# Average pooling in 3D: the closing barrier and the clearing of semaphores run beside the last stores

## The chip, the cores and the metric

The kernel runs on one core of a Trainium2 chip. The metric is the device time of one execution in microseconds, as the median of several runs; smaller is better. The profile is that of one execution, and its span goes from the first to the last instruction of the kernel. The device time is longer than the span: the profiled execution took 93.1 us and its span is 91.3 us.

## The reference

The input `x` is a float32 array of 8 x 32 x 32 x 32 x 32 (batch, channels, depth, height, width). The output is the mean over windows of 2 x 2 x 2 that do not overlap, an array of 8 x 32 x 16 x 16 x 16:

```python
out_d = d // kernel_size
...
for i in range(out_d):
    for j in range(out_h):
        for k in range(out_w):
            ...
            result[:, :, i, j, k] = np.mean(window, axis=(-3, -2, -1))
```

So 33.55 MB are read and 4.19 MB are written, and each element read takes part in one sum.

## The kernel before

Batch and channels make 256 rows, taken as two tiles of 128 rows, one row on each of the 128 partitions of on-chip memory. A row's depth, height and width lie behind each other. The list `plan` cuts each tile's rows into pieces along the depth: six pieces of 4 MB (8192 floats in each partition), and two buffers more that are filled by two loads of 2 MB each. There are ten loads in all (line 77), all issued from SyncE, called SP here, into a pool of five buffers named `tin`. A load into a buffer that was used before waits until VectorE is done with the old contents.

For each piece VectorE runs three instructions, in `pool_unit`: it adds neighbours in depth (line 58), then neighbours in width (line 62), and then neighbours in height with the factor 0.125 (line 65); the last writes its part of `obuf`. The result of all pieces stays in two buffers `obuf` until whole runs of it are stored. There are three stores (line 86), issued from SP as well: 2 MB for the first tile, and 1.75 MB and 0.25 MB for the second. Each waits for the VectorE instruction that completes its source. The third can be issued only when the last piece is finished.

Semaphores connect the engines. Each load or store adds 16 to a semaphore, in sixteen single counts, when its data has landed. Nine semaphores are used in the body, numbers 99 to 107; 101 counts VectorE's instructions, and the other eight belong to transfers and are used in turn. The three stores add to 102, 103 and 104, each of which an earlier load has already raised to 16, so that a store has landed when its semaphore is at 32.

What the change is about lies behind the body. `tc.close()` and `tc.compile()` (lines 95 and 96) generate a closing block, and the profile puts its instructions down to line 96. In order:

- SP waits, in four instructions of two semaphores each, for all eight transfer semaphores, stores included; a drain of SP then waits for VectorE's count.
- A barrier over all five engines. ScalarE (ACT), TensorE (PE), VectorE (DVE) and SP each run a drain that adds 1 to semaphore 96, and then wait for semaphore 97. GpSimd (POOL) waits until 96 is at 4, takes the 4 away, and adds 4 to 97; each of the others takes 1 of it and goes on.
- GpSimd, after a drain, clears the range of semaphores 99 to 107 with one instruction.
- The same barrier again.

The kernel itself already reorders the program once: lines 101 to 108 take the first load out of the body and put it ahead of the opening barrier. Instructions of the opening carry line 125, that of the program's construction.

Of the kernel before, what the change touches and what calls it, by code (L numbers as in the profile page):

```python
# [1 line left out]

# [4 lines left out]

F32 = mybir.dt.float32
KF = 256

@with_exitstack
def pool_rows(
    ctx: ExitStack,
    tc: tile.TileContext,
    x: bass.AP,
    kernel_size: int,
    out: bass.AP,
):
    nc = tc.nc  # L20
    assert kernel_size == 2, "only kernel_size == 2 supported"

    B, C, D, H, W = x.shape
    P = nc.NUM_PARTITIONS
    assert (B * C, D, H, W) == (2 * P, 32, 32, 32)
    add = mybir.AluOpType.add

    xv = x.rearrange("b c d h w -> (b c) (d h w)")  # L30
    ov = out.rearrange("b c d h w -> (b c) (d h w)")

    pool_in = ctx.enter_context(tc.tile_pool(name="pin", bufs=5))
    pool_out = ctx.enter_context(tc.tile_pool(name="pout", bufs=1))
    obuf = [pool_out.tile([P, 16 * KF], F32, name=f"obuf{t}") for t in range(2)]
    dummy = pool_out.tile([P, 1], F32, name="dummy")

    plan = [
        (0, 0, (32,)),
        (0, 32, (32,)),
        (0, 64, (32,)),
        (0, 96, (32,)),
        (1, 0, (32,)),
        (1, 32, (32,)),
        (1, 64, (16, 16)),
        (1, 96, (16, 16)),  # L50
    ]

    def pool_unit(buf, t, k0, kb):

        od = kb // 8
        a = buf.rearrange("p (o dd e) -> p o dd e", o=od, dd=2)
        b = buf[:, :od * 1024]
        nc.vector.tensor_add(  # L58
            out=b.rearrange("p (o e) -> p o e", o=od), in0=a[:, :, 0], in1=a[:, :, 1])
        bv = b.rearrange("p (e ww) -> p e ww", ww=2)  # L60
        c = buf[:, od * 1024:od * 1536]
        nc.vector.tensor_add(out=c, in0=bv[:, :, 0], in1=bv[:, :, 1])  # L62
        cv = c.rearrange("p (j hh k) -> p j hh k", hh=2, k=16)
        o0 = k0 * KF // 8
        nc.vector.tensor_tensor_reduce(  # L65
            out=obuf[t][:, o0:o0 + od * 256].rearrange("p (j k) -> p j k", k=16),
            in0=cv[:, :, 0], in1=cv[:, :, 1],
            scale=0.125, scalar=0.0, op0=add, op1=add, accum_out=dummy[:, :],
        )

    for t, k0, parts in plan:
        tin = pool_in.tile([P, 32 * KF], F32, tag="tin", name="tin")
        views = []
        o = 0
        for kb in parts:
            v = tin[:, o * KF:(o + kb) * KF]
            nc.sync.dma_start(
                out=v, in_=xv[t * P:(t + 1) * P, (k0 + o) * KF:(k0 + o + kb) * KF])
            views.append((v, k0 + o, kb))
            o += kb  # L80
        for v, k, kb in views:
            pool_unit(v, t, k, kb)

    for t, k0, kb in [(0, 0, 16), (1, 0, 14), (1, 14, 2)]:
        nc.sync.dma_start(
            out=ov[t * P:(t + 1) * P, k0 * KF:(k0 + kb) * KF],
            in_=obuf[t][:, k0 * KF:(k0 + kb) * KF],
        )

def kernel(tc: tile.TileContext, x: bass.AP, kernel_size: int, out: bass.AP):
    nc = tc.nc
    pool_rows(tc, x, kernel_size, out)
    tc.close()
    tc.compile()  # L96
    blocks = nc.main_func.blocks

    opening, program = blocks[0].instructions, blocks[tc.starting_block_idx].instructions
    load = next(i for i in program if isinstance(i, mybir.InstDMACopy))
    assert load.engine == nc.sync.engine
    barrier = next(
        n for n, i in enumerate(opening)
        if i.engine == load.engine and isinstance(i, mybir.InstDrain))
    program.remove(load)
    opening.insert(barrier, load)

# [1 line left out]
_INS = ['x', 'kernel_size']  # L112
_OUTS = [((8, 32, 16, 16, 16), 'float32')]

_NUMBERS = {'kernel_size': 2}

# [26 lines left out]
```

## Time and profile before

| what | value |
|---|---|
| time, median of 3 runs | 93.52 us (93.45 to 93.53) |
| the profiled execution | 93.1 us |
| span in the profile | 91.3 us |
| VectorE busy | 64.0 us, 70% of the span |
| bytes over the span | 413 GB/s |
| VectorE waiting for loads | 20.5 us, 6 times |
| start of the last store's issue on SP | 85.2 us |
| issue to landing of the three stores | 36.2, 8.8 and 5.1 us |

The profile has one row for each engine that did work and one for the transfers, with one digit for each fortieth of the span (2.28 us): 9 means that nine tenths or more of that slice were busy. Semaphore instructions and drains are not counted as busy. They are still in the trace, as instructions of an engine's queue: a "q" behind the engine's name (SPq, POOLq) marks them, and their duration is that of the execution, without the wait ahead of it. The groups of one line, asked for within a window of time, show how many ran, their shortest, median and longest duration in nanoseconds, and the first and last start.

### The profile page before, as it was taken

To read this page: it belongs to the slowest core of one execution; us is meant where nothing else is said; L and a number is where in the kernel's file an instruction comes from. 1 tells how busy PE (TensorE), PEld (TensorE's weight loads), DVE (VectorE), ACT (ScalarE), POOL (GpSimd) and SP (SyncE) were. 2 spreads that over 40 slices of the span, in tenths; PEclk is the share of its full clock that TensorE was granted. 3 is DMA by queue.
4 is the path that set the end of the run, shared out by engine and by line. 5 is a ranking of instruction groups with operands and counts; after the bars stand their busy time and mean duration, and the time that the engine had idled before them with its cause. 6 is when DMAs were issued, how large, how long until landed. Compare 5 with 4: busy or idle time off the path is not lost.

```text
span 91.3 us, 103 instructions
## 1 busy us (share of the span) xinstructions
DVE 64.0 (70%) x40; POOL 0.2 (0%) x4
## 2 busy tenths in 40 slices
DVE  0000079974999299939995699749999999999300
POOL 0000000000000000000000000000000000000000
DMA  8998799999997899999997999989999999999992
GB/s 230 459 445 373 344 445 459 459 459 459 459 445 344 373 445 459 459 459 459 459 431 330 388 459 459 459 345 459 445 395 423 459 431 395 409 409 436 427 395 84
DMA packets 1872, 37.75 MB, mean 413 GB/s; under 512 B 208, under 2 KB 208, under 8 KB 336
## 3 DMA queue, kind: packets, MB, share of 16 engines
q1 hardware_dynamic: 1872, 37.75, 97.2%
HBM read 33.55 MB, written 4.19 MB: 413 GB/s over the span
## 4 chain that ended last, share of the span: by engine, by line
DMA 58%; DVE 35%; issue 0%; DVEq 0%
DMA tin<-in_x_dram 58%; DVE tin L58 19%; DVE tin L62 10%; DVE obuf L65 6%; DVE dummy L65 0%; DVEq L96 0%
## 5 line engine op out<-in xcount | busy, mean ns | idle before, releaser
L58 DVE TENSOR_TENSOR tin<-tin 128x4096 f32<-128x4096 f32 (+1 forms) x10 | 35.7, 3569 | 20.5 <-DMA tin<-in_x_dram 20.5
L62 DVE TENSOR_TENSOR tin<-tin 128x2048 f32<-128x2048 f32 (+1 forms) x10 | 18.6, 1864 | 0.3
L65 DVE CUSTOM_DVE_ANT_1 obuf<-tin 128x1024 f32<-128x1024 f32 (+1 forms) x10 | 10.1, 1011 | 0.3
L65 DVE DVE_READ_ACCUMULATOR2_ANT dummy<- 128x1 f32 x10 | 0.8, 82 | 0.0
L125 POOL MEMSET const-bfloat16-1.0<- 128x1 bf16 x1 | 0.1, 101 | 0.0
L125 POOL MEMSET const-uint8-127<- 128x1 uint8 x1 | 0.1, 101 | 0.0
L125 POOL MEMSET const-float32-0.0<- 128x1 f32 x1 | 0.1, 98 | 0.2 <-issue 0.2
L125 POOL MEMSET const-float32-1.0<- 128x1 f32 x1 | 0.1, 98 | 0.0
## 6 DMA issues: line engine op xcount, KB each, us to landing
tin<-in_x_dram SPq DMA_DIRECT2D x6, 4096.0 KB, 34.9
tin<-in_x_dram SPq DMA_DIRECT2D x4, 2048.0 KB, 38.0
out_dram<-obuf SPq DMA_DIRECT2D x1, 2048.0 KB, 36.2
out_dram<-obuf SPq DMA_DIRECT2D x1, 1792.0 KB, 8.8
out_dram<-obuf SPq DMA_DIRECT2D x1, 256.0 KB, 5.1
```

The source lines that it names most:

```text
L58: nc.vector.tensor_add(out=b.rearrange("p (o e) -> p o e", o=od), in0=a[:, :, 0], in1=a[:, :, 1])
L62: nc.vector.tensor_add(out=c, in0=bv[:, :, 0], in1=bv[:, :, 1])
L65: nc.vector.tensor_tensor_reduce(out=obuf[t][:, o0:o0 + od * 256].rearrange("p (j k) -> p j k", k=16), in0=cv[:, :, 0], in1=cv[:, :, 1], s ...
L125: nc = _bacc.Bacc("TRN2", target_bir_lowering=False, num_devices=1)
```

## The change

After the program has been generated, the changed kernel edits the closing block. The purpose is that the barrier and the clearing don't stand behind the landing of the stores.

- SP no longer waits for the three store semaphores on its way into the closing barrier. It still waits there for the semaphores of the loads and for VectorE's count.
- The first barrier stays. Behind it GpSimd clears the semaphores in two pieces, 99 to 101 and 105 to 107, each with a drain ahead of it, and leaves out 102, 103 and 104.
- The second barrier is removed.
- SP ends with three instructions, one for each store: it waits until the semaphore has 32 and subtracts 32, so that it is back at zero.

```diff
+    closing = blocks[-1].instructions
+    stores = [
+        i for i in program
+        if isinstance(i, mybir.InstDMACopy) and "out_" in i.outs[0].memref]
+    kept = [u.id for i in stores for u in i.sync_info.on_update]
+    final = next(
+        i for i in closing
+        if i.engine == nc.sync.engine and isinstance(i, mybir.InstDrain))
+    waits = {w.id: w for w in final.sync_info.on_wait}
+    closing[closing.index(final)] = mybir.InstDrain(
+        name=final.name, engine=final.engine, ins=[], outs=[], is_reset_sema=False,
+        sync_info=mybir.SyncInfo(
+            on_wait=[w for n, w in waits.items() if n not in kept], on_update=[]))
...
+    while len(closing) > reset:
+        closing.pop()
+    n = first
+    while n < stop:
+        m = n
+        while m < stop and m not in kept:
+            m += 1
+        if m > n:
+            closing.append(mybir.InstDrain(
+                name=nc.get_next_instruction_name(), engine=nc.gpsimd.engine, ins=[], outs=[],
+                is_reset_sema=True, reset_range_start=n, reset_range_stop=m))
+            nc.gpsimd.sem_clear(range(n, m))
+        n = m + 1
+    for n in kept:
+        w = waits[n]
+        closing.append(mybir.InstEventSemaphore(
+            name=nc.get_next_instruction_name(), engine=nc.sync.engine, ins=[], outs=[],
+            sync_info=mybir.SyncInfo(
+                on_wait=[w],
+                on_update=[mybir.SyncUpdate(
+                    sync_type="semaphore", id=n, ant_name=w.ant_name,
+                    update_mode="sem-sub-imm", update_value=w.wait_value)])))
```

`reset` is the place of the drain ahead of the clearing; the loop that pops removes all from there on, the second barrier included. At this point the waits of SP's drain are still in one list; they are split into instructions of at most two waits later, when the program is lowered.

## The prediction

> **What bounds the kernel now.** I read the page first, then busy times by stretch around the end, then the waits of the SP queue, then the closing block (line 96) in short windows. The page:
>
> ```profile
> span 91.3 us, 103 instructions
> DMA  8998799999997899999997999989999999999992
> DMA 58%; DVE 35%; issue 0%; DVEq 0%
> out_dram<-obuf SPq DMA_DIRECT2D x1, 256.0 KB, 5.1
> ```
>
> The row of tenths says that the transfers fill the span up to the last slice, which is at two tenths: there the DMA has stopped and something else runs. The chain of waits ends with the last VectorE work at 85.2 us, so it does not reach the end; what follows is the last store, 5.1 us from issue to landing. Busy times of the two stretches after VectorE's end (columns: stretch, length, DVE, POOL, PE clock, DMA share, GB/s):
>
> ```profile
> 85.20:90.30 5.10, 0.00 (x0) 0.00 (x0) 1.00 0.80 338
> 90.30:91.30 1.00, 0.00 (x0) 0.00 (x0) 1.00 0.00 0
> ```
>
> For 5.1 us the stores alone move, then for 1.0 us nothing moves and nothing computes. Who waits there:
>
> ```profile
> SPq L96 <- DMA out_dram<-obuf: 4.8, 1, 4.8
> ```
>
> SP stands in the closing block 4.8 us for the stores, and everything else in that block is behind it. The closing block by windows (count, durations in ns, first and last start), first 90.3 to 90.7, then 91.0 to 91.4:
>
> ```profile
> L96 SPq EVENT_SEMAPHORE  x4: 28/28/28, 90.3 to 90.5; - x4
> L96 SPq DRAIN  x2: 7/7/7, 90.6 to 90.6; - x2
> ...
> L96 POOLq EVENT_SEMAPHORE_RANGE_CLEAR  x1: 92/92/92, 90.9 to 90.9; - x1
> L96 POOLq DRAIN  x1: 34/34/34, 91.1 to 91.1; - x1
> L96 SPq EVENT_SEMAPHORE  x1: 17/17/17, 91.3 to 91.3; - x1
> L96 PEldq EVENT_SEMAPHORE  x1: 51/51/51, 91.3 to 91.3; - x1
> ```
>
> In nanoseconds from the trace's records: the last of the sixteen counts of the last store comes at 90.312 us. [...] So the tail behind the last landing is 91.319 - 90.312 = 1.007 us, all of it sequencer work in series.
>
> The time counts more than the span: the profiled execution took 93.1 us with a span of 91.3. The trace's semaphore records go on after the span: semaphore 2 counts nine times from 91.554 to 92.079, then nearly all semaphores are written once (91.978 to 92.640), then semaphore 2 counts nine times from 92.864 to 93.221. That is 1.90 us after the span, and it agrees with the 1.8 us difference. I take it that the time ends with it.
>
> [...] the waits last 28 ns but start 61 to 69 ns apart, so I price by starts. [...] Here the last packet ends at 89.958 and the last count is at 90.312, 0.35 us that the change leaves alone.
>
> **The change part by part.**
>
> 1. The waits for the store semaphores (102, 103, 104) leave SP's entry to the closing block. Left are three waits (load semaphores, and loads landed by 80.5) and a drain on VectorE's count (reached at 85.210). SP finishes issuing the last store at 85.227 + 0.332 = 85.559. Four starts of about 65 ns bring it to the barrier near 85.8. Cost nothing: the 4.75 us of store flight to 90.312 hide it.
> 2. The first barrier moves there. From SP's drain to its release it takes 90.816 - 90.646 = 0.17 us. Queued behind SP's wait are no transfers; all issues are done. Hidden.
> 3. GpSimd clears twice (99 to 101, 105 to 107) in place of once. One drain and clear took 91.028 - 90.837 = 0.19 us; two, 0.38. GpSimd is done near 86.4. Hidden by the same flight, and SP does not wait for it.
> 4. The second barrier is gone: from the clear's end at 91.028 to 91.319, 0.29 us off the path.
> 5. SP gets three instructions that wait for one store semaphore each and subtract 32. Those for 102 (complete at 85.409) and 103 (89.815) are past before the last landing. The one for 104 starts, as SP's wait did before, 17 ns after 90.312, at 90.329. This form on SP is not in the trace; nearest rows are GpSimd's wait with subtraction, 17 ns, and SP's wait for two, 28 ns. I take 22: end 90.351. The bounds move this by 6 ns.
>
> Sum for the span: from 91.319 to 90.351, 0.97 us off. For SP's own end: 91.273 - 90.351 = 0.92 us. Instructions: ACT, PE and DVE lose two each, GpSimd one, SP none: 103 - 7 = 96.
>
> 6. What follows the span. Only SP is late now; the others enter the runtime's barrier some 4 us early. In the first nine counts before, the steps are 34, 205, 44, 23, 99, 39, 34 and 47 ns; in the second nine 35, 38, 43, 24, 98, 38, 34, 47. So in the first pass all but one step is bare hand-over, and the 205 waited for a late engine. The engines are not named in these records. I read the order as PE, ACT, GpSimd, DVE, SP and back: the long step at the fifth count is the turn, and straight behind it (91.978) begins the writing of 207 to 255, the last of five blocks. So SP is the turning point, counting at 91.860, which is 0.587 us after its last instruction; the four counts ahead of it can all be made while stores fly. How long SP needs from its last instruction to its count, the trace doesn't show: at most those 0.587. PE, the first in the chain, needed 91.554 - 91.319 = 0.235; ACT at most 91.588 - 91.277 = 0.311; GpSimd 91.793 - 91.231 = 0.562. I take 0.28 for SP, between PE and ACT. Its count comes at 90.351 + 0.28 = 90.63 in place of 91.86: 1.23 us earlier, and all behind it follows unchanged. With 0.235 it is 1.27, with 0.587 it is 0.92.
>
> **Forecast:** 93.52 - 1.23 = 92.29 us.
>
> **The rivals.**
>
> A, as worked out: 92.29. For it: the end is one line of hand-overs, and the change leaves one wait of it behind the last landing.
>
> B, SP's way into the runtime's barrier is as slow as GpSimd's, or the order is another one and an early engine saves nothing: only 0.92 is gained, 92.60. For it: that 0.56 exists on one engine, and SP's own is unseen. Against: the two nearest sequencers are under 0.32.
>
> C, SP's drain in the barrier holds until its stores have landed. Then the barrier begins near 90.33 in place of 90.646, 0.32 earlier, and GpSimd's two clears run behind it: its end, with a second drain and clear, comes at 91.028 - 0.32 + 0.19 = 90.90, against 91.231 before, 0.33 gained: 93.19. Against it stands the opening, where the first load is issued ahead of SP's drain:
>
> ```profile
> L125 SPq DRAIN  x1: 142/142/142, 0.4 to 0.4; - x1
> ```
>
> That drain is over at 0.57 us while the load lands at 12.1.
>
> D, slower: the barrier, the clears and the engines that stand in the runtime's barrier disturb the stores. The 5.1 us stretch would have to grow by 1.23 / 5.1 = 24% to lose the gain; at 40% it is 2.0 us, 93.52 - 1.23 + 2.0 = 94.3. For it: during the flight nothing else runs before. Against: these are some dozen semaphore operations, and loads with VectorE's counting beside them moved over 400 GB/s in most slices.
>
> **How the numbers follow.** A 0.66, B 0.22, C 0.06, no change (the time doesn't end where I think) 0.02, D 0.04. Range: below, SP at 0.2 gives 92.21, and the three times before spread by 0.08, with the profiled run 0.4 lower, so down to 92.05; above, B's 92.60 and a tenth more. C, no change and D stay out, 0.12. Faster 0.94, same 0.02, slower 0.04.
>
> **What would show it.** Right: a span near 90.35 and 96 instructions; line 96's barrier and both clears between 85.6 and 86.6; behind the last landing one SP wait and nothing else of the kernel; semaphore 2's first four counts before the landing and the fifth about 0.28 us after SP's end. Wrong: a barrier at 90.3 (C); a fifth count 0.5 us or more after SP's end (B); a last landing later than about 5.1 us after its issue (D). If the span falls by 0.97 and the time hardly moves, the time doesn't end where I put it.

## The result, and the profile after

The changed kernel takes 91.85 us (median of 5 runs, 91.73 to 92.03), beside 93.45 us of the kernel before on the same chip (5 runs, 93.24 to 93.53). The ratio is 0.9838, with a 95% interval of 0.9819 to 0.9858: 1.33 to 1.69 us less. The forecast of 92.29 us had the direction and the mechanism; the gain was larger than it said, and the time lies under its range of 92.05 to 92.7.

The page of the changed kernel:

```profile
span 86.4 us, 90 instructions
...
DMA  8979997999979999799979999799999999998999
...
out_dram<-obuf SPq DMA_DIRECT2D x1, 256.0 KB, 5.4
```

The span of 86.4 us is no measure of the gain. The six instructions that the edit makes itself (SP's drain, GpSimd's two drains, SP's three last waits) carry no line of the source, and the page leaves them out. So the last instruction it knows is GpSimd's second clear, and 4 us of stores lie behind its span. The last line has the last store at 5.4 us from issue to landing, beside 5.1 before; in this execution the last landing came at 90.603 us, beside 90.312. Whether the change delays the stores is taken up below.

The groups of the closing barrier (line 96) and of the clears (line 144) in the changed kernel; count, duration in ns, first and last start:

```profile
L96 POOLq EVENT_SEMAPHORE  x2: 17/17/17, 85.9 to 86.0; - x2
...
L96 SPq DRAIN  x1: 7/7/7, 85.9 to 85.9; - x1
L96 SPq EVENT_SEMAPHORE  x1: 17/17/17, 86.0 to 86.0; - x1
...
L96 PEldq EVENT_SEMAPHORE  x1: 51/51/51, 86.0 to 86.0; - x1
```

```profile
L144 POOLq EVENT_SEMAPHORE_RANGE_CLEAR  x2: 46/48/51, 86.2 to 86.3; - x2
```

What stood from 90.6 to 91.3 us stands from 85.9 to 86.4, four microseconds ahead of the last landing. The same kernel with the source line given to the edit's instructions (below, after_traced) shows what is left at the end. Its page, and its line 96 and its stretches near the last landing:

```profile
span 90.6 us, 96 instructions
```

```profile
L96 SPq EVENT_SEMAPHORE  x1: 17/17/17, 90.6 to 90.6; - x1
```

```profile
85.20:90.30 5.10, 0.59 (x2) 0.00 (x0) 1.00 0.89 375
90.30:90.60 0.30, 0.00 (x0) 0.00 (x0) 1.00 0.00 0
```

One instruction of the kernel runs behind the stores, in place of the whole line before. The idle microsecond at the end of the span has shrunk to 0.3 us: the last packet ends at 90.212 us and the last count of its semaphore comes at 90.561. This stretch from the last packet to the last count was 0.35 us before, and it is 0.34 to 0.36 us in all thirteen traces, so the change does leave it alone.

What follows the span is read from the trace's records of semaphore 2. It counts nine times in a first pass and nine times in a second, and from the end of the first pass on most of the other semaphores are written once each: in the change the counts come at 86.315 to 90.928 and 91.755 to 92.111 us, the writes at 90.882 to 91.531. "The runtime's barrier" and "the runtime's reset", in the prediction and in what was expected of the runs, are the author's names for the counts and the writes; the records name no program and no engine, and they don't have the values written. I call **tail** the time from the last count of the last store's semaphore to the eighteenth and last count of semaphore 2. It is 2.909 us before (90.312 to 93.221) and 1.508 after (90.603 to 92.111), 1.401 less. The device times of the two profiled executions, 93.1 and 91.99 us, both lie 0.12 us under that last count. In all thirteen traces of this document the difference is 0.11 to 0.12 us, so the time does end there.

### The profile page after: what moved, and what is told of

It reads as the page before. It is cut to its first block, busy times and chain, and to the rows that moved or that the text cites. A ratio compares the mean times of both kernels' runs of the same rounds, so it can differ in the third digit from the quotient of the medians.

```text
span 86.4 us, 90 instructions
## 1 busy us (share of the span) xinstructions
DVE 64.0 (74%) x40; POOL 0.2 (0%) x4
## 4 chain that ended last, share of the span: by engine, by line
DMA 61%; DVE 37%; issue 0%; DVEq 0%
DMA tin<-in_x_dram 61%; DVE tin L58 21%; DVE tin L62 11%; DVE obuf L65 6%; DVE dummy L65 0%; DVEq L96 0%
```

## The experiments

Each row has the time of the kernel before on the same chip beside it. All variants of the changed kernel give their instructions a source line, as after_traced does. "Early" is how many counts of semaphore 2 come ahead of the last landing, "first late" how long behind the landing the next one comes, "9 to 10" the step between its two passes. The last four columns are of the one profiled execution of each kernel.

| kernel | time, us | before, us | ratio, 95% | early | first late, ns | 9 to 10, ns | tail, us |
|---|---|---|---|---|---|---|---|
| before | | 93.45 | | 0 | 1242 | 785 | 2.909 |
| the change | 91.85 | 93.45 | 0.9819 to 0.9858 | 4 | 162 | 827 | 1.508 |
| after_traced | 92.01 | 93.39 | 0.9823 to 0.9874 | 4 | 162 | 832 | 1.514 |
| second_hidden | 92.02 | 93.39 | 0.9822 to 0.9874 | 4 | 167 | 788 | 1.476 |
| late_first | 92.16 | 93.39 | 0.9841 to 0.9889 | 4 | 312 | 828 | 1.662 |
| wait_pool | 92.59 | 93.39 | 0.9880 to 0.9932 | 2 | 615 | 830 | 2.089 |
| stores_last | 93.10 | 93.29 | 0.9969 to 0.9991 | 0 | 991 | 787 | 2.660 |
| no_second | 93.09 | 93.29 | 0.9967 to 0.9987 | 0 | 785 | 829 | 2.715 |
| wait_act | 92.15 | 93.29 | 0.9857 to 0.9902 | 1 | 183 | 830 | 1.695 |
| wait_dve | 92.17 | 93.29 | 0.9852 to 0.9897 | 3 | 245 | 829 | 1.673 |
| wait_pe | 92.50 | 93.36 | 0.9877 to 0.9931 | 0 | 359 | 786 | 1.859 |
| pe_pad | 91.94 | 93.36 | 0.9826 to 0.9864 | 4 | 163 | 784 | 1.466 |
| second_wait_only | 91.84 | 93.36 | 0.9818 to 0.9857 | 4 | 160 | 787 | 1.467 |

In every row the gain in the tail lies inside the interval of the measured gain. The times missed the expected ones by up to 0.19 us; many of these were built on the 91.85 us of the first comparison, which the same kernel with source lines did not repeat (92.01). So kernels are compared by their tails where the times can't tell them apart.

**after_traced: does the tail hold all of the gain?**

```diff
         name=final.name, engine=final.engine, ins=[], outs=[], is_reset_sema=False,
+        debug=final.debug,
...
                 name=nc.get_next_instruction_name(), engine=nc.sync.engine, ins=[], outs=[],
+                debug=final.debug,
```

> The changed kernel with one difference: the instructions that the edit makes carry line 96, so that the profile shows them. Both theories expect the changed kernel's time, 91.85 us, and a tail (last count of the last store's semaphore to the last count of semaphore 2) of 1.51 us against 2.91 before. Theory 1 (the whole gain lies in the tail: one SP wait behind the landing, then SP's short way of about 0.13 us into the runtime's barrier, then a turn of 44 ns in place of 99): 96 instructions, the last SP wait 17 ns behind the last count. The time is then 1.40 us under before's, and the last landing lies within the same 0.3 us as before's. Theory 2 (the rest, 0.2 us of the 1.60 in the medians, comes from stores that land earlier): the last landing is 0.2 us earlier than before's 90.31, near 90.1 us.

Measured: 92.01 us against 93.39, so 1.38 us less, with 1.395 less in the tail and the last landing at 90.561 us. One execution can't settle where the stores land, but the spans of all runs can: less the instructions behind the landing (0.034 us here, 1.007 before), they put it at 90.62 us on average in the four runs of this kernel and at 90.64 in the eleven of the kernel before. The last landing is not earlier, and the second theory falls. The 0.2 us by which the first comparison's 1.60 exceeds 1.40 did not come again with this kernel, and 1.40 lies within that comparison's interval; no run shows them to be a part of the change. The last landing wanders by more than 0.2 us from run to run: the eleven runs of the kernel before spread from 93.13 to 93.75 us, and their spans go along, 91.3 at 93.13 and 92.0 at 93.75. In this profiled execution the last store was issued at 85.817 us in place of 85.227, and it landed within 0.25 us of before all the same. It came 0.52 us behind the landing of the store ahead (90.039), beside 0.50 before (89.815). In the trace of before the last store's packets, 2 KB each, run from 88.704 us on, 3.48 us behind the start of its issue, and those of the store ahead, 14 KB each, from 84.444 to 89.306; so for 3.48 of the 5.1 us from its issue to its landing only that store's data moved.

**second_hidden: is it the removal of the second barrier?**

```diff
+    second = list(closing[reset + 2:])
     while len(closing) > reset:
         closing.pop()
...
+    for i in second:
+        closing.append(i)
     for n in kept:
```

> The changed kernel with the second barrier put back, between GpSimd's two clears and SP's three waits for the stores. Theory 1 (what counts is only what stands behind the landing): no change against the changed kernel, 91.85 us and a tail of 1.51 us, since the second barrier takes 0.3 us of a flight of 4.7. Rival (the gain came from dropping the second barrier): 0.29 us or more comes back, 92.15 us and a tail of 1.80.

Measured: 92.02 us beside 92.01 without the barrier; tail 1.476, if anything less. Both barriers are over early (line 96, up to 90 us):

```profile
L96 SPq EVENT_SEMAPHORE  x6: 17/17/28, 85.6 to 86.7; - x6
L96 POOLq EVENT_SEMAPHORE  x4: 17/17/17, 85.9 to 86.5; - x4
```

Removing the second barrier is worth nothing measurable once the waits stand behind it.

**stores_last and no_second: the parts alone, in the old place.** The first only reorders SP's waits in the kernel before; the second only removes the second barrier from it.

```diff
...
+        on_wait=[w for n, w in waits.items() if n not in kept], on_update=[]))
+    for n in kept:
+        place += 1
+        closing.insert(place, mybir.InstEventSemaphore(
+            name=nc.get_next_instruction_name(), engine=nc.sync.engine, ins=[], outs=[],
+            debug=final.debug,
+            sync_info=mybir.SyncInfo(on_wait=[waits[n]], on_update=[])))
```

> The kernel before with one edit: SP waits for the loads' semaphores and VectorE's count first and for the stores last, ahead of both barriers and the clear, which stay where they were. Theory 1 (each sequencer instruction behind the landing costs 61 to 69 ns): three waits and a drain leave the path, the barrier's drain on SP starts about 0.08 us behind the last count in place of 0.33, tail 2.91 - 0.25 = 2.66, 93.2 us. Rival (waits that are satisfied cost nothing): tail 2.91, 93.45 us.

Measured: 93.10 against 93.29 us, tail 2.660, 0.25 less, as the first theory had it. From 90.5 to 90.7 us its line 96 has one wait and one drain on SP where the kernel before had four and two:

```profile
L96 SPq EVENT_SEMAPHORE  x1: 28/28/28, 90.5 to 90.5; - x1
L96 SPq DRAIN  x1: 7/7/7, 90.6 to 90.6; - x1
L96 POOLq EVENT_SEMAPHORE  x1: 17/17/17, 90.7 to 90.7; - x1
```

Satisfied waits that stand behind a late one were not free here: three of them and a drain took 0.25 us.

```diff
...
+    while len(closing) > reset + 2:
+        closing.pop()
```

> The kernel before with the second barrier removed and nothing else; the first barrier and the clear still stand behind the stores' landing. Theory 1 (the runtime's barrier takes GpSimd's count third, and GpSimd's way there is about 0.55 us from the end of its clear): the third count comes at 91.03 + 0.55 = 91.58 in place of 91.79, 0.21 us gained, tail 2.70, 93.24 us. Rival (the whole barrier's 0.29 us comes off, as the span shows it): tail 2.62, 93.16 us. In both it is a small part of the 1.40 that the full change takes off the tail.

Measured: 93.09 against 93.29 us, tail 2.715. The third count of semaphore 2 comes 1.244 us behind the landing in place of 1.481, and GpSimd's clear ends 0.717 behind it, so GpSimd's way is 0.527 us. The 0.29 us that the span loses are not what the tail loses, 0.194 (the interval of the time, 0.12 to 0.31 us, holds both): the barrier's removal moves GpSimd's count of semaphore 2, the third, 0.24 us earlier, and 0.04 is given back between the passes (below). The two parts in the old place give 0.25 + 0.19 = 0.44 of the 1.40 us. The rest needs what neither of them does: barrier, clear and GpSimd's way of 0.53 us laid beside the flight.

**late_first: what does an instruction behind the landing cost?**

```diff
-    for n in kept:
+    for n in reversed(kept):
```

> The changed kernel with SP's three waits in reverse order: the store that lands last is waited for first, so that two waits that are long satisfied stand behind the landing. Theory 1 (sequencer instructions in series behind the landing cost their distance between starts, 61 to 69 ns): +0.13 us, tail 1.64, 91.98 us. Rival (they cost their shown duration, 17 ns): +0.03 us, tail 1.54, 91.88 us.

Measured: 92.16 us, tail 1.662, 0.148 more than after_traced. Its line 96 from 90.6 us on:

```profile
L96 SPq EVENT_SEMAPHORE  x3: 17/17/17, 90.6 to 90.8; - x3
```

By the records they start at 90.620, 90.696 and 90.770: 75 ns apart, where plain waits lay 61 to 69 apart. The rival, who priced by the shown 17 ns, falls. Each of the two instructions shows 17 ns and adds 74 to the tail.

**wait_pool, wait_act, wait_dve, wait_pe: the order of semaphore 2's counts and each engine's way to its own.** The three waits go to another engine, for instance:

```diff
-            name=nc.get_next_instruction_name(), engine=nc.sync.engine, ins=[], outs=[],
+            name=nc.get_next_instruction_name(), engine=nc.gpsimd.engine, ins=[], outs=[],
...
```

> The changed kernel with the three waits for the stores on GpSimd in place of SP. Theory 1 (what follows the landing is the late engine's own way into the runtime's barrier, then the counts behind it): GpSimd's way was 0.56 us before against SP's 0.13, and three hand-overs come behind it (44, 23 and the turn of 99 in place of 44): +0.43 + 0.07 + 0.055 = 0.55 us on the changed kernel, 92.40 us, tail 2.06. Rival (all sequencers are alike and only the number of waits behind the landing counts): 91.85 us, tail 1.51.

> The changed kernel with the three waits for the stores on ScalarE in place of SP. Theory 1 (order of the runtime's barrier: TensorE, ScalarE, GpSimd, VectorE, SP and back): ScalarE is second, so counts three to five and the long turn come behind it, about 0.11 + 0.055 us, and its own way may be between SP's 0.13 and the bound of 0.31: +0.17 to +0.34 us, tail 1.68 to 1.85, 92.0 to 92.2 us; in the records one count of semaphore 2 comes early and eight behind the landing. Rival (the place in the order doesn't matter): 91.85 us, tail 1.51, with ScalarE as good as SP.

> The changed kernel with the three waits for the stores on VectorE in place of SP. Theory 1 (order TensorE, ScalarE, GpSimd, VectorE, SP and back): VectorE is fourth, so three counts come early and six behind the landing, with SP's hand-over of 23 ns and the long turn of 99: +0.08 us plus what its own way takes over SP's 0.13, at most 0.17 more, so tail 1.59 to 1.76, 91.93 to 92.1 us. Rival (the place in the order doesn't matter): 91.85 us, tail 1.51.

> The changed kernel with the three waits for the stores on TensorE in place of SP. Theory 1 (order TensorE, ScalarE, GpSimd, VectorE, SP and back): TensorE is first, so no count of semaphore 2 comes before the landing, all nine come behind it (about 35, 38, 43, 24, 99, 38, 34, 47 ns apart), and TensorE's own way is at most the 0.24 us of the kernel before: first count at most 0.33 us behind the landing, tail 1.75 to 1.88, 92.25 to 92.4 us. Rival (the place in the order doesn't matter): four counts before the landing, tail 1.51, 92.0 us.

The number of early counts gives the order outright: none when TensorE waits, one with ScalarE, two with GpSimd, three with VectorE, four with SP. So the order is TensorE, ScalarE, GpSimd, VectorE, SP, and the remaining four of the nine counts come behind SP's. The kernel's last instruction at the end of wait_pool, and then of wait_pe:

```profile
L96 POOLq EVENT_SEMAPHORE  x1: 17/17/17, 90.7 to 90.7; - x1
```

```profile
L96 PEldq EVENT_SEMAPHORE  x1: 51/51/51, 90.5 to 90.5; - x1
```

Both kernels have the same single wait behind the landing, and their tails are 0.58 and 0.35 us longer than after_traced's. From the end of that last instruction to the engine's own count it took 0.575 us on GpSimd (0.615 less its end at 0.040), 0.279 on TensorE (0.235 in the kernel before), 0.198 on VectorE, 0.145 on ScalarE, and 0.128 on SP (after_traced). With another engine the long turn at SP also came back, 98 to 99 ns in place of 44. The tails of all four lie where the first theory put them, GpSimd's 0.03 us above. The times of three are above what it said: wait_pool's by 0.19 us, wait_dve's by 0.07 and wait_pe's, 92.50, by 0.10, with 92.17 to 92.71 in its four runs. By their spans, wait_pe's stores landed some 0.16 us later on average than those of the kernel before on that chip (90.72 and 90.56 us).

**pe_pad and second_wait_only: a step of 0.04 us, and the shortest version.** Of the first ten kernels three had 785 to 788 ns between the passes of semaphore 2, and seven had 827 to 832. Of the semaphores that are written around this step, the block of 7 to 53 comes last: its first write is 214 ns behind the ninth count before (92.293 us) and 258 in the change (91.186). I read it as TensorE's; the records don't say so.

```diff
+    for _ in range(2):
+        closing.append(mybir.InstDrain(
+            name=nc.get_next_instruction_name(), engine=nc.tensor.engine, ins=[], outs=[],
+            is_reset_sema=False, debug=final.debug))
     for n in kept:
```

> The changed kernel with two drains more at the end of TensorE's instructions, as many as the second barrier gave it. In the runs so far, the step from the ninth to the tenth count of semaphore 2 is 785 to 788 ns in the three kernels that keep the second barrier and 827 to 832 in the seven that drop it, and TensorE's first write in the runtime's reset comes 214 or 260 ns behind the ninth count. Theory 1 (how many instructions TensorE has ahead of the runtime's part sets it): 786 ns, TensorE's first write after 214, tail 1.47. Rival (something else of the second barrier, such as the other engines' instructions): 828 ns, tail 1.51. The time can't tell 0.04 us; both say about 92.0.

Measured: 784 ns, the first write of that block 212 ns behind the ninth count, tail 1.466. The two drains in the trace:

```profile
L96 PEldq DRAIN  x2: 8/8/8, 86.2 to 86.3; - x2
```

Two idle drains on TensorE bring back the 0.04 us that dropping its barrier instructions had cost. wait_pe says the same: it drops the second barrier too, but puts three waits on TensorE, and it has 786 ns and a first write after 214. So instructions added on TensorE alone are enough, and they move this block, as they should if it is TensorE's; why they matter stays open.

second_wait_only puts the second barrier back, as second_hidden does, and leaves out the subtraction:

```diff
-                on_wait=[w],
-                on_update=[mybir.SyncUpdate(
-                    sync_type="semaphore", id=n, ant_name=w.ant_name,
-                    update_mode="sem-sub-imm", update_value=w.wait_value)])))
+                on_wait=[w], on_update=[])))
```

> The kernel with the second barrier put back beside the flight, and SP's three waits without the subtraction[...]. It is the version that the runs point to as the shortest: both barriers hidden (TensorE's step of 786 ns) and one plain wait behind the landing. Theory 1 (waits are all that is left, subtraction on the same instruction is part of its 17 ns): tail 1.47 to 1.48 as with the subtraction, 92.0 us. Rival (the subtraction costs up to the 15 ns by which satisfied waits with it, 75 ns apart, exceed the 61 to 69 of those without): tail 1.46.

Semaphores 102 to 104 stay at 32 here. In the traces of before and of the change each of them is written once more behind the span, at 92.397 to 92.410 and at 91.228 to 91.241 us; with what value, the records don't show.

Measured: 91.84 us, tail 1.467; the first late count at 160 ns, 167 in second_hidden with the subtraction. Those 7 ns don't price the subtraction, since without it two of the three waits, those for 102 and 104, became one instruction:

```profile
L96 SPq EVENT_SEMAPHORE  x2: 17/22/28, 89.9 to 90.4; - x2
```

The last wait lasts 28 ns here and 17 there, so the two kernels differ by more than the subtraction. This version's tail is 0.04 us shorter than the change's; the times, 91.84 against 93.36 and 91.85 against 93.45 in separate comparisons, can't tell them apart. Its wait view also names the wait, which the kernels with a subtraction put down to SP itself:

```profile
SPq L96 <- DMA out_dram<-obuf: 3.8, 2, 3.3
```

## Why the prediction was right in kind and short in size

- **What bounds the end: right.** It read a tail of sequencer work in series behind the last landing, and a time that ends with semaphore 2. Both hold; the gain is in the tail to within the measurement.
- **Steps 1 to 3, hidden at no cost: right.** Barrier and clears lie at 85.9 to 86.4 us, where it put 85.8 to 86.4. The clears were even shorter, 46 and 51 ns for three semaphores each, where the one for nine had taken 92. The stores' flight was not disturbed, by the landings under D below.
- **Step 4, the second barrier 0.29 us off: right as a part of the span, and no part of the gain once the waits stand last.** second_hidden has it and is as fast.
- **Step 5: right.** SP's last wait starts 17 ns behind the last count, and its subtraction is recorded 34 ns behind it. From the landing to SP's own end it is 0.034 us in place of 0.961, so 0.927 less; the prediction had 0.92. 96 instructions, as counted.
- **Step 6, what follows the span: the step that failed.** Its path was right: four counts come early, and SP's, the fifth, sets the time, as the four runs with another engine confirm. Two of its terms were not. It put SP's way to its count of semaphore 2 at 0.28 us, between TensorE's and ScalarE's bound; SP takes 0.128 (90.765 less 90.637, which is the landing and after_traced's 34 ns), so 0.459 is gained against the 0.587 of before, not 0.31. Those 0.587 were a wait: GpSimd's count came 0.562 us after its last instruction, and SP's could only follow it. The neighbours' figures, bounds from above, gave no bound from below, and SP is quicker than every one of the four. The other term was left out: "all behind it follows unchanged". The step behind SP's count is 44 ns and not 99, which gives 0.055. It is 98 or 99 in the seven first passes in which VectorE counts just ahead of SP, and 43 to 45 in the six in which VectorE had counted some 3 to 4 us before; why, no run shows. A third term goes the other way, the 0.04 us by which the step between the passes is longer (827 ns in place of 785). The sum is 0.927 + 0.459 + 0.055 - 0.040 = 1.401 us; 93.45 - 1.40 would be 92.05, the very edge of the range.
- **The range: too narrow at the lower end.** Its end took SP at 0.2 us and 0.16 us more for the wander of the times, of which it had three, 0.08 us apart, and one 0.4 lower. The runs since have spread by 0.3 (this kernel, 5 runs) and 0.6 us (40 runs of before, 93.06 to 93.68), and the spans of the 40 spread by 0.6 as well (91.3 at 93.06, 91.9 at 93.68). So the wander lies within the span and not behind it. It is in when the last store lands: in the five runs of second_hidden, which has one wait behind the landing, the spans are 90.4 to 90.9 us. From 92.05 to the 91.85 measured, 0.2 us are left. No run shows a further effect of that size; after_traced gained 1.38 us in time and 1.395 in the tail. That the 0.2 are this wander is likely and not shown, as the spans of the changed kernel end ahead of its landing.
- **The rivals.** B needed SP to be as slow as GpSimd; GpSimd's 0.53 to 0.58 us are its own, as wait_pool and no_second show. C, a drain that holds for stores, is refuted: SP's drain in the barrier is over at 85.9 us, and barrier and clears at 86.4, with 4 us of the stores' flight still to come. D, disturbed stores: in the profiled executions of the changed kernel and its variants the last landing is at 90.41 to 90.79 us, and at 90.31 in that of before, a quick one (93.1 us). The averages over the runs, from the spans as above, are within 0.1 us of those of the kernel before on the same chip in every kernel that shows its landing, but for wait_pe's 0.16.

## What to carry to other kernels

Whatever must wait for the last store should be one wait, and the last thing that its engine does; barriers, clears and satisfied waits go ahead of it, where a flight like the 4.7 us here hides them. Let that one wait stand on SP: it was the quickest of the five to its count of semaphore 2 (0.13 us, beside 0.145 to 0.58), and it counts fifth there, so the other four engines' counts were made while the stores flew. Price instructions of the sequencer by the distance of their starts (61 to 75 ns here, where the profile shows 17 to 28), and what follows the span by the semaphore records, as the span alone said 0.97 us here, and the time said 1.4.

## What was not expected of the hardware

- Each engine's way from its last instruction to its count of semaphore 2 differs by more than four times: SP 0.116 to 0.134 us, ScalarE 0.145, VectorE 0.198, TensorE 0.235 to 0.279, GpSimd 0.53 to 0.58.
- With two instructions fewer at the end of TensorE's part of the kernel, the last block of semaphore writes, 7 to 53, starts about 45 ns later (258 to 266 ns behind the ninth count in seven kernels, 212 to 215 in six); two idle drains, or three waits, on TensorE take that back.
- A clear of three semaphores took 46 to 51 ns, one of nine 92.
